# A 12 KB first load, a shifted row pitch and a smaller last load in a max-pooling kernel that streams 134 MB

## The chip, the cores and the metric

The kernel runs on one core of one Trainium2 chip. The metric is the device time of one execution in microseconds (us), as the median of several runs.

Some terms. VectorE is the engine that does the reductions; the 16 DMA engines move data between the memory (HBM) and the working memory of the core. A load or store is *issued* when an instruction puts it into a DMA queue (SPq and ACTq in the lines below are the two engines that do so), and it *lands* when its last byte has arrived. A *packet* is one DMA engine's record of one piece; here it is one partition's row of one load or store, so 128 packets make up a load. A line of the profile gives start and duration in us, engine, line of the kernel, instruction, output and input with their sizes, count, and in brackets how long the engine waited before it and for what.

## The reference

An adaptive max pooling along the last axis. With these sizes every output is the maximum of 16 neighbouring inputs, called a *window* below.

```python
batch, channels, length = 32, 256, 4096      # x: float32, 134.2 MB
output_size = 256                            # result: 32 x 256 x 256 float32, 8.4 MB
for i in range(output_size):
    start, end = int(i * length / output_size), int((i + 1) * length / output_size)
    result[:, :, i] = np.max(x[:, :, start:end], axis=-1)
```

There is one comparison per input element, so the first question is how fast 142.6 MB can pass.

## The kernel before

Seen as rows of windows, each of the 128 partitions has 16,384 windows of 64 B. They are read in two groups; in each group a partition reads one contiguous stretch of memory, so the stretch's length is the distance in memory (the *row pitch*) between neighbouring partitions.

```python
CHUNK, GAP, FIRST, LOADS_A, LOADS_B, LESS = 1024, 152, 128, 9, 6, 4   # lines joined
group_a = [FIRST] + [CHUNK] * (LOADS_A - 1) + [CHUNK - LESS]          # 9340 windows
last = total - sum(group_a) - LOADS_B * CHUNK                         # 900
group_b = [CHUNK] * LOADS_B + [last]                                  # 7044 windows

ring = pool.tile([P, 2 * (CHUNK + GAP) * W], fp32, ...)               # two slots of 1176 windows
kept = pool.tile([P, total - last], fp32, ...)                        # results stay here to the end
...
            if n == FIRST:
                nc.sync.dma_start(out=ring[:, CHUNK * W : (CHUNK + n) * W], in_=xn)
                pooled(dst, CHUNK, n)
            else:
                low = n_loads % 2 * (CHUNK + GAP)
                moved = n_loads // 2 % 2
                at = low + moved * GAP
                nc.sync.dma_start(out=ring[:, at * W : (at + n) * W], in_=xn)
                if n != last:
                    cut = CHUNK - GAP if moved else GAP
                    parts = [(0, cut), (cut, n)]
                    for u, v in parts if moved else parts[::-1]:
                        pooled(dst[:, u:v], at + u, v - u)
                else: ...                                             # final reduction, into the ring
...
nc.scalar.dma_start(out=og[:, full : full + last], in_=last_kept)     # the last store, other queue
tc.no_sync_barrier()
for dst, src in stores:                                               # the two big stores
    nc.sync.dma_start(out=dst, in_=src)
```

Two ideas carry the argument. First, GAP: a slot is a little longer than a chunk, and successive chunks in a slot are placed alternately at its start and at its end. The next load therefore needs only the larger piece of the reduction (872 of 1024 windows) to be over and can be issued before the whole chunk is reduced. Second, the stores are held back to the end, where they run beside the last reduction.

## Time and profile before

| | before |
|---|---|
| time, median (3 runs) | 334.97 us |
| span of the profiled run | 333.2 us |
| VectorE busy | 276.5 us, 83% |
| the two DMA queues, share of the 16 engines | 98.8% + 0.3% |
| data moved over the span | 142.61 MB, 428 GB/s |

The last two rows say most: 16 engines at 99% can only be made faster by fewer bytes, shorter packets or fewer pauses.

### The profile page before, as it was taken

What the parts mean: (1) busy time and instruction counts of PE and PEld (TensorE: products, weight loads), DVE (VectorE), ACT (ScalarE), POOL (GpSimd) and SP (SyncE); (2) the same over time, 40 slices, a digit from 0 to 9 for tenths busy, and PEclk for the clock granted to TensorE, in tenths of its full rate; (3) what the DMA queues carried; (4) which work ended last, traced back from release to release, by engine and by line L of the source; (5) the groups of instructions that cost most, each with busy time, mean ns of one, the idle gap of its engine ahead of it and who ended that gap; (6) DMA issues with size and microseconds to landing.
All of it is one profiled execution on the core that took longest, in us unless ns stands there. A gap on an engine that the chain in (4) does not pass through costs nothing.

```text
span 333.2 us, 113 instructions
## 1 busy us (share of the span) xinstructions
DVE 276.5 (83%) x32; POOL 0.2 (0%) x4
## 2 busy tenths in 40 slices
DVE  2009979797997979799797979979797998979993
POOL 0000000000000000000000000000000000000000
DMA  9898989899898989899898989899898989899987
GB/s 378 378 504 378 504 378 504 378 409 472 378 504 378 504 378 504 378 417 464 376 502 377 504 378 496 386 425 456 378 504 378 504 378 504 378 458 443 393 386 339
DMA packets 2880, 142.61 MB, mean 428 GB/s; under 512 B 320, under 2 KB 320, under 8 KB 448
## 3 DMA queue, kind: packets, MB, share of 16 engines
q1 hardware_dynamic: 2736, 142.15, 98.8%
q10 hardware_dynamic: 144, 0.46, 0.3%
HBM read 134.22 MB, written 8.39 MB: 428 GB/s over the span
## 4 chain that ended last, share of the span: by engine, by line
DMA 57%; DVE 36%; DVEq 5%; issue 0%; SPq 0%
DMA ring<-in_x_dram 57%; DVE kept L56 36%; DVEq L145 5%; SPq L85 0%
## 5 line engine op out<-in xcount | busy, mean ns | idle before, releaser
L56 DVE TENSOR_REDUCE kept<-ring 128x152 f32<-128x2432 f32 (+3 forms) x31 | 261.4, 8473 | 51.6 <-DMA ring<-in_x_dram 51.6
L56 DVE TENSOR_REDUCE ring<-ring 128x900 f32<-128x14400 f32 x1 | 15.1, 15141 | 0.0
L131 POOL MEMSET const-bfloat16-1.0<- 128x1 bf16 x1 | 0.1, 102 | 0.0
L131 POOL MEMSET const-uint8-127<- 128x1 uint8 x1 | 0.1, 101 | 0.0
L131 POOL MEMSET const-float32-0.0<- 128x1 f32 x1 | 0.1, 99 | 0.2 <-issue 0.2
L131 POOL MEMSET const-float32-1.0<- 128x1 f32 x1 | 0.1, 98 | 0.0
## 6 DMA issues: line engine op xcount, KB each, us to landing
ring<-in_x_dram SPq DMA_DIRECT2D x1, 8160.0 KB, 24.0
ring<-in_x_dram SPq DMA_DIRECT2D x1, 7200.0 KB, 21.6
out_dram<-kept SPq DMA_DIRECT2D x1, 4670.0 KB, 32.4
out_dram<-kept SPq DMA_DIRECT2D x1, 3072.0 KB, 18.1
ring<-in_x_dram SPq DMA_DIRECT2D x1, 1024.0 KB, 4.6
out_dram<-ring ACTq DMA_DIRECT2D x1, 450.0 KB, 4.2
ring<-in_x_dram SPq DMA_DIRECT2D x14, 24.0
```

What stands on the lines that cost most here:

```text
L56: nc.vector.reduce_max(out=dst, in_=ring[:, at * W : (at + n) * W].rearrange("p (n w) -> p n w", w=W), axis=mybir.AxisListType.X,)
L131: nc = _bacc.Bacc("TRN2", target_bir_lowering=False, num_devices=1)
L145: with _tile.TileContext(nc) as tc:
```

## The change

The intent is to shorten what follows the last load, by making the last load smaller (900 -> 836 windows) and taking these windows up front in a longer first load. GAP shrinks by 4. Because the sums of the groups change with FIRST, so do the row pitches.

```diff
-    GAP = 152
-    FIRST = 128
+    GAP = 148
+    FIRST = 192
     LOADS_A, LOADS_B = 9, 6
     LESS = 4
```

## The prediction

> **What bounds the kernel now.** I read the busy shares first, then the chain that ended last, then the instructions in order of time, and at the end the DMA packets themselves.
>
> ```profile
> span 333.2 us, 113 instructions
> DVE 276.5 (83%) x32; POOL 0.2 (0%) x4
> ...
> q1 hardware_dynamic: 2736, 142.15, 98.8%
> q10 hardware_dynamic: 144, 0.46, 0.3%
> ```
>
> The two DMA queues together keep the 16 DMA engines busy for 99.1% of the span; VectorE, the only computing engine, is at 83%. The suspect is the transfer, not the reduction. Whether that holds in every stage is shown by the stretches of time (start, loop, tail), where the last two columns are the DMA share and the GB/s:
>
> ```profile
> 5.00:24.00 19.00, 2.29 (x1) 0.00 (x0) 1.00 0.90 390
> 24.00:312.00 288.00, 258.09 (x30) 0.00 (x0) 1.00 1.00 433
> 312.00:332.00 20.00, 16.09 (x2) 0.00 (x0) 1.00 0.98 419
> ```
>
> In the loop the engines never pause: share 1.00 at 433 GB/s. In the tail, which holds the stores of the results beside the last reduction, it is still 0.98. (The view books a packet where it ends, so a short stretch errs by a packet; the 0.90 of the first row is partly that.) The instructions in order of time show the rhythm and the tail:
>
> ```profile
> 257.06 17.28 DVE L56 TENSOR_REDUCE kept<-ring 128x872 f32<-128x13952 f32 x2 [2.08 <-DMA ring<-in_x_dram]
> 276.41 17.28 DVE L56 TENSOR_REDUCE kept<-ring 128x872 f32<-128x13952 f32 x2 [2.07 <-DMA ring<-in_x_dram]
> 291.50 21.91 SPq L114 DMA_DIRECT2D out_dram<-kept  x2
> 295.75 17.28 DVE L56 TENSOR_REDUCE kept<-ring 128x872 f32<-128x13952 f32 x2 [2.07 <-DMA ring<-in_x_dram]
> 312.95 15.14 DVE L56 TENSOR_REDUCE ring<-ring 128x900 f32<-128x14400 f32 x1
> 328.12 0.37 ACTq L111 DMA_DIRECT2D out_dram<-ring  x1
> ```
>
> A chunk of 1024 windows (64 KB per partition) lands every 19.35 us (276.41 - 257.06) and is reduced in 17.28, so VectorE waits 2.07 us each time. The chain that ended last alternates "24 us load, 14.7 us reduction", which looks like a latency chain. It isn't one: the load issued 14.7 us after a landing queues behind the other slot's load, which needs another 19.35 - 14.7 = 4.65 us. That is the slack of the ring.
>
> The packet list of the trace closes the case: a 65,536 B packet takes 2.418 us (median of 1792; 5th percentile 2.418, 95th 2.427), one of 8,192 B 0.309 us, 37,360 B 1.382, 24,576 B 0.912, 3,600 B 0.141. All of these are bytes / 27.2 GB/s plus about 8 ns. Between 1.74 us, when the first packet starts, and 331.8, when the last ends, an engine goes from one packet to the next.
>
> **What the Trainium skill says.** (1) "DMA: Bandwidth & Descriptors", section "Where 436 GB/s comes from", gives a fabric ceiling of 435.2 GB/s for the 16 ports. The trace agrees: 433 GB/s in the loop, 16 x 27.2 = 435 without the 8 ns per packet. So memory is not what limits a packet now. (2) The same page, "Latency and other measured facts", row "HBM row pitch at large powers of two": [...]+4 KiB of padding restores them, +192 B doesn't; the cause is called an inference. The trace before shows no such loss. (3) The same page, "The descriptor swizzle": engine = 8 * (partition >> 6) + ((partition >> 2) & 7), thus neighbouring engines work 4 rows apart. The trace has 8 data packets per engine and load, which fits; which partition each carries isn't recorded. (4) "VectorE: DVE Perf Modes", "The perf-mode tier table": tensor_reduce has only the 1x mode. The trace agrees with one element per 0.96 GHz cycle: (14686 - 2676) ns / (872 - 152) windows = 16.68 ns for a window of 16 elements, plus a fixed 140 ns.
>
> **The change part by part.** The loads still number 17, the stores 3, the reductions 32 over the same 16,384 windows per partition. Bytes and packets are the same: 128 rows x 20 transfers, 142.6 MB. So the sum of the packet times is unchanged to the nanosecond unless a packet of the same size gets slower or an engine pauses. Four places where it could:
>
> *Start.* FIRST 128 -> 192 makes the first load 12 KB per row. It takes 8 packets x (12,288 / 27.2 GB/s + 8 ns) = 3.68 us per engine instead of 2.47, and every later landing is 1.21 us later (524,288 B / 433 GB/s); these bytes are taken from the last load. Its reduction takes 0.14 + 192 x 0.01668 = 3.34 us. New is an overlap: the first load fills windows 1024 to 1216 of the ring, but the second slot now begins at 1024 + 148 = 1172. The second chunk therefore waits for the first reduction: 5.40 + 1.21 + 3.34 = about 10 us. The first chunk is in transfer until 24.7 + 1.2 = 25.9, so about 16 us of slack. Cost: 0.
>
> *Loop.* GAP 152 -> 148 moves 4 windows into the piece that frees a slot: 876 instead of 872, 4 x 16.68 = 67 ns later of 4.65 us slack. The short piece is as much shorter. Cost: 0.
>
> *Tail.* The last load still lands near 312.7 (issue 291.12 + 21.6), as the bytes are the same. The chunk before it lands at 295.73 + 1.21 = 296.94 and takes 17.2 us, so the final reduction starts near 314.15, held by VectorE. It covers 836 windows: 0.14 + 836 x 0.01668 = 14.09 us instead of 15.14. End: 328.25, against 328.09 before. What looks like 1.07 us saved is given back by 1.21 us of later start: +0.15. Is this on the path? Stores of 8.39 MB follow the last load on the engines, 8.39 MB / 433 GB/s = 19.4 us, 312.7 -> 332.1. Before, the last store's packets began at 330.36 on the earliest engine, 6 ns after that engine's end marker of the big store: they were waiting for it. That is 2.24 us after the issue began, while the first load needed 1.0 us from issue to first packet; so up to 1.2 us of slack, and 0.15 fits. Cost: 0 to 0.15.
>
> *Row pitch.* Group A's pitch goes from 9340 x 64 = 597,760 B to 9404 x 64 = 601,856 B: from 256 B short of a multiple of 8 KB to 256 B short of an odd multiple of 4 KB. Group B's goes from 450,816 (256 B over) to 446,720 (4352 B over). By (3), engines are 4 rows apart, and 4 x 4096 is a multiple of 8 KB: the engine offsets modulo 8 KB stay what they were, steps of 1 KB. Only address bits from 16 KB upward change. Neither pitch is a large power of two. Cost: 0 expected, not proved. The output rows keep their offset modulo 256 B (37,360 -> 37,616; 28,176 -> 27,920).
>
> Sum: 0 to +0.15 us; 334.97 -> about **335.05**.
>
> **The rivals.** *A, the pitch matters.* Speaking for it: (2), and the constant of 4 windows that holds the old pitch off an exact multiple of 8 KB, which looks like tuning. Against: packets are at the fabric's pace, the mean of 2.4216 us lies 0.0036 over the median, and the residues are kept. If group A's loads (77 MB, 178 us) lost 5%, the time would be 344. In the good direction at most 0.0036 x 112 packets per engine = 0.4 us is there. *B, the tail is bound by VectorE and the last store's latency.* Then the shorter reduction alone would give -1.05 (333.9), with the later chunk it is +0.15 (335.1). Against: the packets found waiting. *C, the new overlap at the start starves the queue.* The second chunk's issue would have to be over 25 us for that; its wait ends at 10. *D, a smaller GAP stalls the ring*: 0.067 against 4.65 us.
>
> **Range and chances.** Repeats of the old kernel differ by 0.12 us. I put 334.5 at the low end (the 0.4 us of slow packets gone) and 335.9 at the high end (tail shift, another chip, slight conflicts of 0.2%). Faster by over 2% would need 6.7 us, which a transfer at 99% of the engines can't give: 0.01. Slower by over 2% needs rival A: 0.04. Within: 0.95.
>
> **What would show it.** Right: first landing near 6.6 us, chunk landings still 19.35 apart, 65,536 B packets still at 2.418, the final reduction starting near 314.15 without a wait for a DMA and ending near 328.25, DMA share 1.00 in the loop. Wrong: longer packets in one group of loads (A), the last store's packets starting after a pause (B), a gap before the second chunk (C), or a VectorE wait above 2.1 us in the loop (D).

## The result, and the profile after

| | before | after |
|---|---|---|
| time, median of 6 runs | 334.97 us | 335.04 us |
| range | 334.83 to 335.13 | 334.91 to 335.19 |
| ratio | | 1.0002 (0.9989 to 1.0015) |

The two kernels can't be told apart.

The page of the kernel after, its span, engines and DMA queues:

```profile
span 333.3 us, 114 instructions
DVE 276.5 (83%) x32; POOL 0.2 (0%) x4
...
q1 hardware_dynamic: 2736, 142.18, 98.8%
q10 hardware_dynamic: 144, 0.43, 0.3%
```

The packet counts are the same to the packet; 0.03 MB went from the last store (q10) to a big one (q1). The stretches of the kernel after, with the DMA share and GB/s in the last two columns:

```profile
5.00:24.00 19.00, 3.35 (x1) 0.00 (x0) 1.00 1.07 463
24.00:312.00 288.00, 256.76 (x30) 0.00 (x0) 1.00 1.00 432
312.00:332.00 20.00, 16.35 (x2) 0.00 (x0) 1.00 0.96 410
```

The loop stands at share 1.00 as before. The first row counts a packet where it ends, so more than 1 in a short stretch means nothing. The kernel after in order of time, start and tail:

```profile
6.91 3.35 DVE L56 TENSOR_REDUCE kept<-ring 128x192 f32<-128x3072 f32 x1 [6.91 <-DMA ring<-in_x_dram]
26.24 17.28 DVE L56 TENSOR_REDUCE kept<-ring 128x876 f32<-128x14016 f32 x2 [15.97 <-DMA ring<-in_x_dram]
...
277.73 17.28 DVE L56 TENSOR_REDUCE kept<-ring 128x876 f32<-128x14016 f32 x2 [2.08 <-DMA ring<-in_x_dram]
292.89 21.84 SPq L114 DMA_DIRECT2D out_dram<-kept  x2
297.08 17.28 DVE L56 TENSOR_REDUCE kept<-ring 128x876 f32<-128x14016 f32 x2 [2.07 <-DMA ring<-in_x_dram]
314.28 14.08 DVE L56 TENSOR_REDUCE ring<-ring 128x836 f32<-128x13376 f32 x1
328.38 0.37 ACTq L111 DMA_DIRECT2D out_dram<-ring  x1
```

Here is the whole story of the tail. The final reduction became 1.06 us shorter (15.14 -> 14.08), and it starts 1.33 us later (312.95 -> 314.28), because the chunk ahead of it landed later and VectorE went straight from one to the other: there is no wait in brackets. It ends 0.27 us later than before (328.36 against 328.09). From the packet list of the trace, the last data packet ends at 331.83 us before and at 331.92 after; the packets of 65,536 B take 2.418 us before and 2.419 after (medians of 1792).

### The profile page after: what moved, and what is told of

Read it like the earlier page. It is cut to its first block, busy times and chain, and to the rows that moved or that the text cites. A ratio compares the mean times of both kernels' runs of the same rounds, so it can differ in the third digit from the quotient of the medians.

```text
span 333.3 us, 114 instructions
## 1 busy us (share of the span) xinstructions
DVE 276.5 (83%) x32; POOL 0.2 (0%) x4
## 4 chain that ended last, share of the span: by engine, by line
DMA 58%; DVE 36%; DVEq 5%; issue 0%; SPq 0%
DMA ring<-in_x_dram 58%; DVE kept L56 36%; DVEq L145 5%; SPq L85 0%
## 5 line engine op out<-in xcount | busy, mean ns | idle before, releaser
L56 DVE TENSOR_REDUCE kept<-ring 128x148 f32<-128x2368 f32 (+3 forms) x31 | 262.5, 8507 | 51.9 <-DMA ring<-in_x_dram 51.9
L56 DVE TENSOR_REDUCE ring<-ring 128x836 f32<-128x13376 f32 x1 | 14.1, 14076 | 0.0
```

What stands on the lines that cost most here:

```text
L56: nc.vector.reduce_max(out=dst, in_=ring[:, at * W : (at + n) * W].rearrange("p (n w) -> p n w", w=W), axis=mybir.AxisListType.X,)
```

## The experiments

Theory: the 16 DMA engines are the limit from the first packet to the last, and the three edits move things that are hidden beside them. Rivals: A, the row pitch matters; B, VectorE and the last store set the end; C and D, a wait in the ring. Each run is compared with runs of the kernel before in the same rounds.

### VectorE at half its work

```diff
-            in_=ring[...].rearrange("p (n w) -> p n w", w=W),
+            in_=ring[...].rearrange("p (n w) -> p n w", w=W)[:, :, 0 : W // 2],
```

> The changed kernel, each reduction reading only 8 of the 16 elements of a window (wrong results on purpose): VectorE busy falls from 276 to about 140 us, the final reduction from 14.1 to about 7.1 and it starts with the landing of the last load near 312.7. Theory (DMA engines bound): 334.7 to 335.1, the time does not move. Rival B (VectorE sets the end): about 8.5 us less, 326.5.

Measured: 335.10 us, ratio 1.0001 (0.9987 to 1.0014), wrong results as meant. The run in order of time:

```profile
296.88 8.75 DVE L56 TENSOR_REDUCE kept<-ring 128x876 f32<-128x7008 f32 x2 [10.61 <-DMA ring<-in_x_dram]
312.77 7.12 DVE L56 TENSOR_REDUCE ring<-ring 128x836 f32<-128x6688 f32 x1 [7.14 <-DMA ring<-in_x_dram]
319.92 0.37 ACTq L111 DMA_DIRECT2D out_dram<-ring  x1
```

VectorE has half its work, waits 10.6 us in a chunk of the loop, and issues the last store 8.46 us earlier (319.92 instead of 328.38): not a tenth of a microsecond comes of it. This settles rival B for any shortening of the tail reduction. The intent of the change, a shorter last reduction, could not have paid.

### The tail delayed

An extra reduction, its result unused, ahead of the final one, of 28 windows and of 150:

```diff
+                    pooled(scratch[:, 0:28], at, 28)
                     pooled(last_kept, at, n)
```

> The changed kernel with one extra reduction of 28 windows (0.61 us) ahead of the final one, its result unused. Theory (the last store's packets wait behind the big store, so a later issue is hidden while it comes within the slack): the last store is issued near 329.0 instead of 328.38 and the time stays at 335.04, within 0.2 us. Rival B (VectorE and the last store set the end): 335.65.

> As the run before, with 150 windows (2.64 us). Theory: issue near 331.0, first packet of the last store 1.0 us later at the earliest, so the slack is used up and the rest shows: 336.2 to 336.9, that is 1.2 to 1.9 us and not 2.64. Rival B: 337.7. Full hiding (335.0) would show the slack to be larger than I take it to be.

Measured: 335.08 us, ratio 1.0000 (0.9988 to 1.0013), for the short delay, which put the issue of the last store at 328.86, 0.48 us later than in the changed kernel; 335.92, 1.0027 (1.0013 to 1.0040), for the long one. The tail of the long one:

```profile
314.31 2.64 DVE L56 TENSOR_REDUCE scratch<-ring 128x150 f32<-128x2400 f32 x1
...
316.87 14.08 DVE L56 TENSOR_REDUCE ring<-ring 128x836 f32<-128x13376 f32 x1
330.98 0.37 ACTq L114 DMA_DIRECT2D out_dram<-ring  x1
```

The last store's first packet follows its issue by 0.87 us here (331.85), where the engines had run dry; in the changed kernel it came 1.88 us after its issue, behind the big store. An issue 2.60 us later costs 0.9, so about 1.7 us of slack lay in the tail (about 1.5 by the profiled runs, where the last data packet ends at 333.06 instead of 331.92). I had expected 1.2 to 1.9 us of loss: the slack is larger than I took it to be. That the issue needs 0.87 us and not 1.0 is a small part of it; the rest is not accounted for.

### The first load alone

The kernel before with FIRST = 192.

> The kernel before with the first load at 192 windows, GAP left at 152. Theory (the DMA engines bound every stage, the tail store waits behind the big store): 335.0, within 0.2 us of both kernels; final reduction starts near 314.2 to 314.3 as in the changed kernel, so the later start comes from the first load alone. Rival B (tail bound by VectorE and the last store): 335.1 to 335.3.

Measured: 335.08 us, ratio 1.0000 (0.9987 to 1.0013). The final reduction starts at 314.15, so the later start in the tail is the first load's doing. The last load and the pitches depend on FIRST, so this run has those of the changed kernel too: only GAP is left out.

### The pitch at exact multiples of 8 KB and at 512 KiB

```diff
-    LESS = 4
+    LESS = 0
```

> The kernel before with LESS = 0: group A's pitch is 598016 B, an exact multiple of 8 KB (73 x 8192), group B's 450560 B (55 x 8192), so that neighbouring engines' rows agree in address bits up to 32 KB. Theory that only the residue within 8 KB can matter and was kept by the change: either no effect (335.0, 64 KB packets at 2.418 us) because the fabric is the limit, or clearly longer packets and a time over 340. Rival A in its strong form (any large aligned pitch hurts): over 340. No effect here means that the pitch step of the change can have had none.

Measured: 334.81 us, ratio 0.9996 (0.9981 to 1.0012); packets of 65,536 B at 2.418 us. The constant LESS, which looks like tuning against an aligned pitch, makes no difference here that can be told from the noise. For a harder case, both groups of 8192 windows:

```diff
-    group_a = [FIRST] + [CHUNK] * (LOADS_A - 1) + [CHUNK - LESS]
-    last = total - sum(group_a) - LOADS_B * CHUNK
-    group_b = [CHUNK] * LOADS_B + [last]
+    group_a = [FIRST] + [CHUNK] * 7 + [CHUNK - FIRST]
+    last = 900
+    group_b = [912] * 4 + [911] * 4 + [last]
```

> Both groups at 8192 windows, a row pitch of exactly 512 KiB (one load more, of the same bytes). Rival A[...]: packets of 64 KB up to twice 2.418 us and a time of 500 to 640 us. Theory that the fabric is the limit whatever the pitch: 335 to 336. It tells whether a pitch can bound this kernel at all.

Measured: 343.83 us, ratio 1.0272 (1.0253 to 1.0292). That is neither what I expected nor a halved rate. The stretches before and after 140 us of this run show where it went:

```profile
24.00:140.00 116.00, 103.68 (x12) 0.00 (x0) 1.00 1.00 433
140.00:320.00 180.00, 155.57 (x20) 0.00 (x0) 1.00 0.99 416
```

Group A, at exactly 512 KiB, runs at the full 433 GB/s. The loss lies after it, where chunks have 911 or 912 windows. Two causes were open: the pitch, in some way peculiar to group B, or the smaller chunks. Moving 4 windows from B to A was refused before it ran (its chunks were computed so that one had 900 windows, as many as the last load, and was taken for it); moving 64 windows ran.

> The run with the pitch of 512 KiB (343.8), with 4 windows moved from group B to group A: pitches of 512 KiB + 256 B and 512 KiB - 256 B, load pieces of the same kind (911 instead of 912 and 911). If the exact 512 KiB pitch cost the 8.7 us: back to 335 to 336, no packets of 2.6 us and more in the loads of group B. If the pieces of 911 windows, or the start of group B at 64 MiB, cost it: 343 to 344 again, with the same long packets.

> The same with 64 windows moved: pitches of 512 KiB + 4 KiB and 512 KiB - 4 KiB, pieces of 904 and 903 windows. Skill's row on pitches: 4 KiB of padding restores the rate, so 335 to 336. If pieces or the start of group B cost it: 343 or more.

Measured with 64 windows moved: 342.83 us, ratio 1.0221 (1.0199 to 1.0243), by its interval unclear against the mark of 2%. Of 8.8 us, 1.0 came back (with chunks of 903 and 904 windows, so not surely by the padding). Most of the loss stayed, which speaks for the chunks.

### GAP: where the ring really stalls

The changed kernel with GAP = 16, 96 and 120 in place of 148.

> The changed kernel with GAP = 16 instead of 148: a slot is freed after 1008 windows, 16.95 us, instead of 876, 14.75; slack 19.35 - 16.95 = 2.4 us, of which about 1.0 is issue to first packet. Theory: 335.0, within 0.2 us, DMA share 1.00 in the loop. Rival D (a later release stalls the ring): 16 loads lose up to 1 us each, over 340.

> The changed kernel with GAP = 96: slots freed after 928 windows, 0.87 us later than with 876, so the lead of each issue over the end of the load ahead falls from 3.5 to 4.1 us to about 2.6 to 3.2. Theory (first packets of a load slow down once the lead is under about 3 us): some of them 0.4 us and more longer, time between 335.5 and 341. If 1 us of lead were enough: 335.0.

> GAP = 120: slots freed 0.47 us later than in the changed kernel, lead about 3.0 to 3.6 us. Theory: 335.0 to 335.5, at most a few slow first packets. If the cost begins right below the tuned lead: over 336.

Measured: GAP = 16: 349.28 us, ratio 1.0420 (1.0379 to 1.0462); GAP = 96: 339.85, 1.0147 (1.0127 to 1.0168); GAP = 120: 335.78, 1.0031 (1.0014 to 1.0047). The first was my plainest miss: I had taken 2.4 us of slack for enough. The chain of waits of the run with GAP = 16, start and duration:

```profile
123.51 24.25 DMA ring<-in_x_dram
147.76 0.02 issue
147.78 16.98 DVE kept L56 x2
164.76 24.39 DMA ring<-in_x_dram
```

The alternation of load and reduction that only looked like a chain before now is one: a pair of chunks takes 24.25 + 0.02 + 16.98 = 41.25 us instead of two times 19.35. The stretch of its loop:

```profile
24.00:312.00 288.00, 243.81 (x29) 0.00 (x0) 1.00 0.98 414
```

The DMA share is still 0.98. The larger part of the loss isn't idle time, it's longer packets. To see which, I took the packet list of each trace and, for every load issued in the loop (from the fourth load on), worked out three things. The *lead* is the time from the start of its issue to the end of the load ahead of it, on the engine that finishes first. The *excess* is how much longer the first packet of the load takes on each engine than bytes / 27.2 GB/s + 8.5 ns, as a mean over the 16 engines. The *idle* is the pause ahead of that packet. (Packets are put to loads by order of start, 128 a load. Excess and idle in the table are means over the loads of the one profiled run, the time is the median of all runs; for GAP 120 the profiled run was the fastest, 335.29 us.)

| run | lead, us: lowest, median | excess, ns | idle, ns | time, us |
|---|---|---|---|---|
| before (GAP 152) | 3.62, 3.78 | 2 | 2 | 334.97 |
| after (GAP 148) | 3.40, 3.49 | 4 | 2 | 335.04 |
| GAP 120 | 3.02, 3.21 | 21 | 6 | 335.78 |
| GAP 96 | 1.60, 2.27 | 178 | 41 | 339.85 |
| GAP 16 | -0.86, 0.85 | 454 | 371 | 349.28 |
| 512 KiB, chunks of 911 and 912 | 0.12, 2.38 | 195 | 152 | 343.83 |
| 512 KiB + 4 KiB, 903 and 904 | 0.19, 2.51 | 210 | 109 | 342.83 |

From run to run the excess follows the lead, whatever the pitch. Once issues come less than about 3 us before the engines need them, loads start on average with slow packets, well before the queue runs dry. It doesn't hold for each load: with GAP = 96, one with a lead of 2.30 us has no excess and one with 2.26 has 0.69 us. Why a short lead makes packets slow isn't shown. For GAP = 16 the sum over its 14 loads is 14 x (0.454 + 0.371) = 11.5 of the 14.2 us, 5.2 of it idle; the rest falls on other packets (the last load's later packets were long as well, some 1.1 us per engine, which I can't explain). A small loss also grows: an engine that falls behind lands its part later, VectorE starts later, the next lead is shorter.

### 512 KiB again, with a long lead

If the lead is the cause, the exact 512 KiB pitch must become harmless once loads are issued early.

```diff
-    CHUNK = 1024
-    GAP = 152
+    CHUNK = 924
+    GAP = 240
...
+    group_a = [FIRST] + [CHUNK] * 8 + [672]
+    last = 848
+    group_b = [918] * 8 + [last]
```

> Both groups again at a row pitch of exactly 512 KiB, but with chunks of 924 and 918 windows and GAP = 240, so that a slot is freed after 684 windows (11.5 us) of a load that takes about 17.4: the next load is issued about 5 us before the engines finish the one ahead, instead of 0.1 to 2.5. Theory (what slowed the 512 KiB runs was this lead, not the pitch): 335 to 336.5, first packets of the loads without excess. Rival A (the pitch cost it): 343 or more, long packets in group B.

Measured: 338.08 us, ratio 1.0091 (1.0076 to 1.0106): of 8.8 us, 5.8 are gone. Of what remains, a pause of 1.80 us is my own making: the chunk of 672 windows is so short that the load after it was issued with a lead of -0.16 us. All other loads of the loop had leads of 4.5 to 7.9, and the mean excess of their first packets was at most 51 ns; the packets of 58,752 B in group B take 2.168 us (median of 1024), which is 58,752 / 27.2 GB/s plus 8 ns. So the pitch of 512 KiB doesn't lengthen the typical packet here. The expected 336.5 was missed, the rest of the difference being not fully accounted for.

### Pitch and last load put back

```diff
-    LESS = 4
+    LESS = 68
```

> The changed kernel with LESS = 68: the 64 windows come out of the last chunk of group A instead of the last load, so both pitches (597760 and 450816 B) and the last load of 900 windows are those of the kernel before; the 12 KB first load and GAP stay. Theory: 335.0, within 0.2 us; final reduction back near 313.0, with the last store issued near 328.2. Rival A: where the pitch had mattered, the time would differ from the changed kernel's by more than 0.3 us.

Measured: 335.79 us, ratio 1.0022 (1.0009 to 1.0036), 0.7 us over what I expected. By the mark set beforehand (more than 0.3 us from the changed kernel) this speaks for rival A. But the kernel before has these very pitches and takes 334.97, so they aren't slow in themselves, and the edit did one thing more: it restores the old pitches but shortens the last chunk of group A to 956 windows. In its packet list the load after that chunk has a lead of 2.50 us, the shortest in the run, and on one engine a first packet with an excess of 0.83 us. That fits the lead; that the one load costs the whole 0.7 us isn't shown.

## Why the prediction was right

**The bound.** Right, and now shown by an intervention: halving VectorE's work leaves 335.10 us. That the measured 335.04 lies 0.01 us from the foretold 335.05 is luck and shows nothing, for the interval of the ratio spans about 0.9 us; the forecast that stood the test is "no change that can be told from the noise".

**Start.** Right in effect. The first landing was foretold near 6.6 us and is at 6.91, the later ones 1.29 to 1.49 us after the old ones instead of 1.21. The first packets of an execution take longer than their bytes (0.50 us over, on average, with 12 KB rows, 0.42 with 8 KB), and this start differs by some 0.2 us between runs (the same load's reduction starts at 6.70 in the run with half the reduction). The wait of the second chunk for the first reduction is hidden: its issue is at 10.29 us, and the engines need it 15 us later.

**Loop.** The verdict held, chunks land 19.35 us apart. The size beneath it was wrong. The prediction set "0.067 against 4.65 us"; the real lead is 3.4 us at its lowest in the changed kernel. The difference is that the first engine is ahead of the last, and VectorE starts later still: for one load of the changed kernel the first engine ends at 63.94, the last at 64.53, and the reduction starts at 64.95. By the table about 3 us of the lead are needed. What is spare is about 0.4 us: 28 windows less of GAP, 0.47 us, already cost 0.8. Four windows, 0.067 us, were harmless for that narrower reason: the verdict was right with far less room than the prediction gave it, and in that part it was lucky.

**Tail.** Right. Final reduction foretold 314.15 to 328.25, measured 314.28 to 328.36, both 0.1 us late because of the start. It wasn't on the path: an issue 0.48 us later costs nothing, and 2.6 us cost 0.9. The slack was about 1.5 to 1.7 us and not "up to 1.2".

**Pitch.** Right: packets of 65,536 B take 2.422 us on average before and 2.421 after, and harsher pitches than the changed one don't lengthen the typical packet while the lead is long. The argument of the prediction, that the residues modulo 8 KB are kept, turned out not to be needed, for with LESS = 0 those residues vanish and the time stays.

**The Trainium skill.** The fabric ceiling of 435.2 GB/s ("DMA: Bandwidth & Descriptors", "Where 436 GB/s comes from") stayed the best single number for this kernel (432 GB/s in the loop after). The row on the pitch was misread, in the prediction and in what was expected of the 512 KiB run: see the list at the end. So that run did not test a pitch at which the page has a loss, and such a pitch (2 MiB and more) stays untested here.

## What to carry to other kernels

Where all DMA engines are busy from the first packet to the last, a shorter reduction or a smaller last load moves nothing; count bytes and packets first, then ask whether an edit creates a pause. In a double-buffered stream, don't take "issued before the queue runs dry" for the condition: read the lead of each issue over the end of the load ahead, and see how long the first packets of a load take compared with the others. Shortening one chunk of a tuned ring can shorten the lead of the load behind it: to 2.50 and to -0.16 us in two runs here.

## What the Trainium skill lacked or had wrong

- "DMA: Bandwidth & Descriptors" doesn't say how far ahead of need a load on a busy queue must be issued. In these runs the first packets of a load were on time within a few ns on average (2 before, 4 after) with leads of 3.4 us and more, 21 ns late at about 3.2, 178 ns at about 2.3 and 454 ns at about 0.9; the time went from 335.0 to 349.3 us.
- The same page, "Latency and other measured facts", gives 207 GB/s for copies between HBM tensors, in tiles of 16 KiB rows, at a row pitch of 512 KiB. The prediction took it for a loss of a half or more from 512 KiB on, which it isn't. The page calls 214 full, and about half of it, 103, belongs to 4 and 8 MiB; its padding by 4 KiB was measured at 4 MiB too. Read so, it doesn't differ: loads from HBM with rows of 64 KB at exactly 512 KiB ran at 433 GB/s in the first group here, and at 434 with 4 KiB more. What the page lacks is a figure for loads from HBM into the core.
- The same page, "Queues, rings and completion order", says that an engine goes round the queues packet by packet. The run with half the reduction agrees from 323.9 us on: one small packet of the last store after each packet of the second big one. But that store was issued at 319.92, and 0.87 us was enough on idle engines; for about 3 us more the engines went on with the first queue alone, until the first big store was over (its last packet ends at 323.34) and one packet of the second had passed. The page doesn't say when a newly filled queue gets its first turn.
